# Hybrid decoder layer on one core: first loads in another order and on other queues, and the last token block's closing arithmetic on other engines

## The chip, the cores and the metric

The kernel runs on one core of a Trainium2 chip. A core has a matrix engine (TensorE, in the profile PE, with its weight loads listed as PEld), a vector engine (VectorE, DVE), an activation engine (ScalarE, ACT), a general engine (GpSimd, POOL) and a queue engine (SyncE, SP). SP, ACT and POOL can each issue DMA transfers; in the profile an issue stands under SPq, ACTq or POOL, and the queues that carry the packets are q1 (SP), q10 (ACT) and q0 (POOL). The metric is device time in microseconds (us), lower is better, as the median of several executions. One further execution is profiled, and all rows of the profile come from that one.

## What is computed

One layer on x of 512 tokens by 1024 channels, float32: a half-step SwiGLU feed-forward (2816 hidden channels), a mixer (RG-LRU channels beside sliding-window attention), and a second half-step feed-forward. Each is wrapped in RMS norms, one on its input and one on its output before the residual add:

```
def rms_norm(x, g):
    y = x * rsqrt(mean(x * x, axis=-1) + 1e-6)
    return y * g
def swiglu(x, w_gu, w_down):
    gate, up = split(x @ w_gu, 2)
    return (silu(gate) * up) @ w_down
x = x + 0.5 * rms_norm(swiglu(rms_norm(x, ffn1_pre_g), ffn1_w_gu, ffn1_w_down), ffn1_post_g)
x = x + rms_norm(mixer(rms_norm(x, mix_pre_g)), mix_post_g)
x = x + 0.5 * rms_norm(swiglu(rms_norm(x, ffn2_pre_g), ffn2_w_gu, ffn2_w_down), ffn2_post_g)
```

Only two places matter here: the first products of the first feed-forward (gate and up, with the gain `ffn1_pre_g`), and the output norm of the last feed-forward with its residual add, for the last 128 tokens.

## The kernel before

Each float32 operand of a product is split into a high part (rounded to the matrix engine's fast float32 form) and a low part (what the rounding left), and each product is three matmuls: high by high, low by high, high by low. The low-by-low one is left out. ACT makes most high parts (`act.copy`, a CAST in the profile), DVE most low parts (a subtraction, TENSOR_TENSOR), POOL a few. Every engine works through its own list in the order in which the code writes it; there is no scheduler that moves instructions, so one late instruction holds everything behind it on its engine.

**The head** (the first 15 us). x comes in as tiles `xn[b][hf]` of 128 tokens by 512 channels (b is the token block, hf the channel half), 256 KB each. PE turns them (transposes through an identity matrix that POOL builds), so that channels lie on partitions: `turn_early` turns the first channel half of blocks 0 and 1 (channel chunks 0 to 3), `turn(0, 4)` and `turn(0, 6)` the second half (chunks 4 to 7). From the turned data in the accumulation memory, `turned_high` makes x's high parts times the gain (xh), `turned_low` the low parts (xl, line 644). The gain is loaded as eight rows of 128 (`g1rows`) and turned by one small matmul (`g_ps`, line 1216), then copied by DVE (line 1282). The root of the mean square is applied later, so the products need only x and the gain.

The weights of the first gate column block (o = 0) and the first up column block (o = F) are loaded as four tiles of 256 KB, `first{o}{i}`, where i = 0 has channel chunks 0 to 3 and i = 1 chunks 4 to 7. The order's names number them: first_88 is gate chunks 0 to 3, first_91 (first_93 after the change) up chunks 0 to 3, first_96 gate 4 to 7, first_98 up 4 to 7. `first_hi` makes their high parts (line 1252, ACT), `first_lo` the low ones (line 1256, DVE, and POOL for the last). `passes(js, ks, part, xpart)` (line 1289) issues the products: js = 0 gate, 1 up; ks the chunks; `lower` is chunks 0 to 3, `upper` 4 to 7. PE's order is: 7 warm-up matmuls (`spin(WARM)`), the early transposes, `spin(2)`, the gate products on the lower chunks, the transposes of the second channel half, the gate's low-x products, the up products on the lower chunks (high, low x, low weight), then all products on the upper chunks. Then blocks 2 and 3 follow in the same way.

A transfer's completion is counted on one of eight semaphores, taken in turn over all transfers that SP and ACT issue. The ninth transfer therefore waits at its issue until the first has landed, the tenth for the second, and so on; the rows of the order show it as a wait on DMAHW0 to DMAHW7.

**The body** (15 to 806 us): feed-forward one, mixer, and feed-forward two, whose weights stream in over SP.

**The tail** (the last 20 us). For each block of 128 tokens, `out_products` ends the down product; DVE adds the part sums (`yp`, line 2126); ACT squares and sums over a row (line 2133, for the last piece line 2129); `tot` collects the mean squares, ACT takes the root (line 2139), DVE the reciprocal `rs` (line 2145); `last` is y times the gain (lines 2136 and 2141); and line 2148 makes the output, `last` times `rs` plus x. The last block has its second channel half in two pieces of 256 channels (i = 1 and 2), so that the last matmuls leave less to do behind them. The output goes out in three transfers for the last block: 256 KB (SP), 128 KB (ACT), 128 KB (SP).

## Time and profile before

| what | us |
|---|---|
| three runs | 835.01, 835.22, 835.38; median 835.22 |
| the profiled execution's own time | 836.39 |
| its span, first to last instruction | 834.6 |
| PE busy | 826.2 (99%) |
| DVE, ACT, POOL busy | 733.8, 520.0, 165.5 |
| mean granted clock of PE | 0.999 |

The profiled execution took 1.2 us longer than the median of the three runs, and 1.8 us of its own time lie outside the span. A row of the timeline gives start and duration in us, engine, line, operation, the tile written and the tiles read, sizes and a count of merged instructions; in square brackets stands how long the engine had been idle and what ended that. A merged row's duration reaches from the first instruction's start to the last one's end, and neighbouring rows of one engine may overlap by the pipeline. PE's records show one instruction per pass: a warm-up matmul has two, a transpose one.

### The profile page before, as it was taken

How to read it: one execution, taken by the hardware profiler on the slowest of the kernel's cores; microseconds unless marked ns; L12 is line 12 of the kernel's file. 1: busy time of each engine (PE TensorE's matmuls, PEld its weight loads, DVE VectorE, ACT ScalarE, POOL GpSimd, SP SyncE). 2: the span in 40 equal slices, each digit the busy share in tenths (PEclk: the TensorE clock that was granted, in tenths of full speed). 3: DMA queues.
4: the chain of work that ended last, by engine and by line, in shares of the span. 5: the costliest groups of instructions: out<-in, count | busy, mean ns of one | idle time of the engine just before them, and what ended most of it. 6: DMA issues, size and time to landing. Idle time of an engine off the chain costs nothing.

```text
span 834.6 us, 11761 instructions
## 1 busy us (share of the span) xinstructions
PE 826.2 (99%) x4190; PEld 701.0 (84%) x4190; DVE 733.8 (88%) x1031; ACT 520.0 (62%) x813; POOL 165.5 (20%) x187
## 2 busy tenths in 40 slices
...
GB/s 254 103 252 244 159 12 308 89 266 259 127 260 180 186 281 230 188 78 94 164 45 51 51 138 15 124 179 253 128 107 240 308 96 250 233 161 261 298 139 102
DMA packets 121835, 144.22 MB, mean 173 GB/s; under 512 B 24168, under 2 KB 76720, under 8 KB 121264
## 3 DMA queue, kind: packets, MB, share of 16 engines
...
q14 instruction: 26, 0.21, 0.1%
HBM read 100.45 MB, written 39.32 MB: 167 GB/s over the span
## 4 chain that ended last, share of the span: by engine, by line
PE 98%; DMA 1%; DVE 0%; SPq 0%; issue 0%; DVEq 0%
PE ab L1026 10%; PE aa L1026 10%; PE db L1026 5%; PE da L1026 5%; PE yaa L1427 3%; PE bb L1026 3%; PE ya L1427 3%; PE ba L1026 3%; PE a_first L1289 3%; PE yda L1427 2%; PE aa L956 1%; PE yab L2016 1%; PE yab L2017 1%; PE yab L2018 1%; PE wo L1942 1%; PE gt L522 1%
## 5 line engine op out<-in xcount | busy, mean ns | idle before, releaser
L1198 POOL DMA_DIRECT2D yr_a<-stage x36 | 31.2, 1015 | 175.7 <-ACT stage L1195 153.8
L1198 POOL DMA_DIRECT2D yp_b<-stage x42 | 36.5, 1070 | 146.3 <-ACT stage L1195 120.0
...
L745 POOL TENSOR_TENSOR acca_r<-acca_r,sq_r 128x512 f32<-128x512 f32 x6 | 9.1, 1509 | 38.2 <-ACT sq_r L552 38.1
L540 PE MATMUL an<-xh_mx,whi_xl 128*128 128x256 f32 x64 | 15.7, 285 | 0.0
L541 PE MATMUL an<-xh_mx,wlo_xl 128*128 128x256 f32 x64 | 15.5, 283 | 0.0
L2136 POOL TENSOR_TENSOR last<-yp,grow 128x512 f32<-128x512 f32 x3 | 3.9, 1291 | 57.0 <-DVE yp L2126 57.0
L2133 ACT ACTIVATE ysq<-yp 128x512 f32<-128x512 f32 (+1 forms) x8 | 4.9, 607 | 15.7 <-DVE yp L2126 15.7
L522 PE MATMUL gt<-xh_mx,whi_gt 128*128 128x512 f32 x32 | 14.2, 443 | 0.0
L1464 POOL DMA_DIRECT2D yp_a<-zy x16 | 8.7, 554 | 25.5 <-DMA rows_a<-yr_a 17.2
L498 ACT ACT_TABLE_LOAD x9 | 11.5, 1283 | 2.4 <-issue 2.3
L522 PE MATMUL pq<-xh_mx,whi_q 128*128 128x512 f32 x32 | 12.8, 400 | 0.0
L524 PE MATMUL gt<-xh_mx,wlo_gt 128*128 128x512 f32 x32 | 12.6, 394 | 0.0
L522 PE MATMUL pgb<-xh_f,whi_bg 128*128 128x512 f32 x32 | 12.6, 393 | 0.0
L523 PE MATMUL gt<-xl_mx,whi_gt 128*128 128x512 f32 x32 | 12.5, 392 | 0.0
L524 PE MATMUL pq<-xh_mx,wlo_q 128*128 128x512 f32 x32 | 12.5, 391 | 0.0
L523 PE MATMUL pq<-xl_mx,whi_q 128*128 128x512 f32 x32 | 12.5, 390 | 0.0
L524 PE MATMUL pgb<-xh_f,wlo_bg 128*128 128x512 f32 x32 | 12.5, 390 | 0.0
L524 PE MATMUL pub<-xh_f,wlo_bu 128*128 128x512 f32 x32 | 12.5, 390 | 0.0
L523 PE MATMUL pub<-xl_f,whi_bu 128*128 128x512 f32 x32 | 12.5, 390 | 0.0
L522 PE MATMUL pub<-xh_f,whi_bu 128*128 128x512 f32 x32 | 12.5, 389 | 0.0
L523 PE MATMUL pgb<-xl_f,whi_bg 128*128 128x512 f32 x32 | 12.5, 389 | 0.0
...
## 6 DMA issues: line engine op xcount, KB each, us to landing
...
raw_ad<-in_ffn_w_down SPq DMA_DIRECT2D x2, 1024.0 KB
xT_hbm<-xT POOLq DMA_DIRECT2D x2, 1024.0 KB, 6.1
```

The source lines that it names most:

```text
L498: act.activation(dummy, eps, func)
L522: pe.matmul(ps, hi[:, k, :], xh, start=start, stop=False)
L523: pe.matmul(ps, hi[:, k, :], xl, start=False, stop=False)
L524: pe.matmul(ps, lo[:, k, :], xh, start=False, stop=stop)
L540: pe.matmul(ps[:, sl], hi[:, k, :], xh, start=k == 0 and not goes_on, stop=False, skip_group_check=True)
L541: pe.matmul(ps[:, sl], lo[:, k, :], xh, start=False, stop=False, skip_group_check=True)
L745: eng.tensor_add(acc, acc, square(part, ALL, f"{self.name}{c}"))
L1026: pe.matmul(b[tb], x[:, blk], w[:, k, :], start=first and q + k + j == 0, stop=q + k == 2 and j == 2, skip_group_check=True)
L1198: pool.dma_start(o, st, accum_op=ALU.add)
L1289: pe.matmul(banks[j][:, sl], ws[j][part][:, k, :], n1.xs[k][xpart][:, sl], start=k == 0 and part == xpart, stop=stop and k == KD - 1)
L1427: pe.matmul(o, x[:, blk], a[:, k, :], start=start and j == 0, stop=stop and j == 2, skip_group_check=True)
L1464: (pool if q % 2 else sync).dma_start(chunks[32 * q:32 * (q + 1), :, i * P:(i + 1) * P], turned[32 * i:32 * (i + 1), :, q])
```

## The change

In the head, x's second channel half for blocks 0 and 1 is loaded over SP and ACT (one tile each) ahead of the up weights' lower chunks, and these are split into two transfers over both queues. The gain's rows leave SP's queue and are issued by POOL after it has built the identity. The gain's small matmul stands after the first two transposes, not after four; the spin behind the transposes is one matmul, not two. The first pair of xh moves from ACT to DVE, and the low part of the up weights' lower chunks from DVE to POOL.

In the tail, for the last block alone: the last piece's square and sum moves from ACT to DVE (a multiplication with a row sum as second output); the small `tot` step that needs only the first piece is written ahead of the last add; the last piece's gain product moves from DVE to POOL; its scaling with `rs` goes to ACT and its residual add to POOL, where one DVE instruction did both.

```diff
--- before.py
+++ after.py
@@ -449,10 +449,9 @@
     load_x(0, 0)
     load_x(1, 0, act)
     load_first(0, 0, act, sync)
-    load_first(F, 0, act)
-    sync.dma_start(g1rows, rows_of("ffn1_pre_g"))
-    for b in range(2):
-        load_x(b, 1)
+    load_x(0, 1)
+    load_x(1, 1, act)
+    load_first(F, 0, act, sync)
     for o in (0, F):
         load_first(o, 1, sync)
     for hf in range(2):
@@ -482,6 +481,7 @@
     dve.memset(ones.bitcast(F32), 1.0)
     ident = const.tile([P, P], F32, name="ident")
     make_identity(nc, ident)
+    pool.dma_start(g1rows, rows_of("ffn1_pre_g"))
 
     def filled(name, w, value):
         t = const.tile([P, w], F32, name=name)
@@ -1212,7 +1212,7 @@
             for i in range(2):
                 j = cc % 2
                 pe.transpose(tp[cc // 2][:, (2 * j + i) * P:(2 * j + i + 1) * P], xn[i][0][:, cc * P:(cc + 1) * P], ident)
-            if cc == 1:
+            if cc == 0:
                 pe.transpose(g1_ps[:, :KD], g1rows, ident[:KD, :KD])
         return dict(zip((0, 2), tp))
 
@@ -1280,7 +1280,7 @@
     g1_ps = bank("g1_ps")
     tps = turn_early()
     dve.tensor_copy(g1, g1_ps[:, :KD])
-    spin(2)
+    spin(1)
     banks = [bank(f"a_first{i}") for i in range(4)]
 
     def passes(js, ks, part=0, xpart=0, stop=False, sl=HALF[0]):
@@ -1298,7 +1298,7 @@
 
     preload(AF.Copy)
     first_hi(0, 0)
-    turned_high(0, 0, tps[0])
+    turned_high(0, 0, tps[0], dve)
     turned_high(0, 2, tps[2])
     first_lo(0, 0)
     turned_low(0, 0, tps[0])
@@ -1311,7 +1311,7 @@
     first_hi(1, 0)
     first_hi(0, 1)
     turned_high(0, 4, tps[4])
-    first_lo(1, 0)
+    first_lo(1, 0, pool)
     first_lo(0, 1)
     turned_high(0, 6, tps[6], dve)
     first_hi(1, 1)
@@ -2123,11 +2123,12 @@
         for i, (dh, c0, c1) in enumerate(pieces[tb]):
             out_products(tb, i, range(f0 + 2 * ((tb, i) in started), f1))
             y = parts[tb, dh][:, c0:c1]
+            if i == 2:
+                dve.tensor_scalar(tot, ss[:, 0:1], 4.0 / D, 4 * EPS, op0=ALU.mult, op1=ALU.add)
             dve.scalar_tensor_tensor(y, place(tb, i), -1.0 if dh else 1.0, y, op0=ALU.mult, op1=ALU.subtract if dh else ALU.add)
             if i == 2:
                 ss_last = small.tile([P, 1], F32, tag="tot", name="ss_last")
-                act.activation(wt(f"ysq{tb}{i}")[:, :c1 - c0], y, AF.Square, accum_out=ss_last)
-                dve.tensor_scalar(tot, ss[:, 0:1], 4.0 / D, 4 * EPS, op0=ALU.mult, op1=ALU.add)
+                dve.scalar_tensor_tensor(wt(f"ysq{tb}{i}")[:, :c1 - c0], y, 1.0, y, op0=ALU.mult, op1=ALU.mult, accum_out=ss_last)
                 dve.scalar_tensor_tensor(tot, ss[:, 1:2], 4.0 / D, tot, op0=ALU.mult, op1=ALU.add)
             else:
                 act.activation(wt(f"ysq{tb}{i}")[:, :c1 - c0], y, AF.Square, accum_out=ss[:, i:i + 1])
@@ -2138,14 +2139,20 @@
         if end:
             act.activation(rs, ss_last, AF.Sqrt, bias=tot, scale=4.0 / D)
             for i, (dh, c0, c1) in list(enumerate(pieces[tb]))[1:]:
-                dve.tensor_mul(last[i], parts[tb, dh][:, c0:c1], grow[dh][:, c0:c1])
+                (dve, pool)[i - 1].tensor_mul(last[i], parts[tb, dh][:, c0:c1], grow[dh][:, c0:c1])
         else:
             dve.tensor_add(tot, ss[:, 0:1], ss[:, 1:2])
             act.activation(rs, tot, AF.Sqrt, bias=eps4, scale=4.0 / D)
         dve.reciprocal(rs, rs)
+        if end:
+            act.activation(last[2], last[2], AF.Copy, scale=rs)
         for i, (dh, c0, c1) in enumerate(pieces[tb]):
             y = parts[tb, dh][:, c0:c1]
-            dve.scalar_tensor_tensor(y, last[i], rs, x_rows[tb][:, dh * T + c0:dh * T + c1], op0=ALU.mult, op1=ALU.add)
+            xr = x_rows[tb][:, dh * T + c0:dh * T + c1]
+            if i == 2:
+                pool.tensor_add(y, last[i], xr)
+            else:
+                dve.scalar_tensor_tensor(y, last[i], rs, xr, op0=ALU.mult, op1=ALU.add)
             (act if end and i == 1 else sync).dma_start(out[0, tb * P:(tb + 1) * P, dh * T + c0:dh * T + c1], y)
```

The first transfers of the two queues, before: eight of SP's rows, then ACT's first four (xn_77 and xn_79 are the first channel half of blocks 0 and 1, xn_78 and xn_80 the second half, xn_81 block 2).

```order
L440 DMA xn_77<-in_x 128x512
L447 DMA first_88<-in_ffn_w_gu 128x2x128
L453 DMA rows<-in_ffn_pre_g 8x128
L440 DMA xn_78<-in_x 128x512
L440 DMA xn_80<-in_x 128x512
L447 DMA first_96<-in_ffn_w_gu 128x4x128 [waits DMAHW0_49]
L447 DMA first_98<-in_ffn_w_gu 128x4x128 [waits DMAHW1_49]
L440 DMA xn_81<-in_x 128x512 [waits DMAHW2_49]
L440 DMA xn_79<-in_x 128x512
L447 DMA first_88<-in_ffn_w_gu 128x2x128
L447 DMA first_91<-in_ffn_w_gu 128x4x128
L498 ACT_TABLE_LOAD
```

And now, seven of SP's rows and ACT's first five:

```order
L440 DMA xn_77<-in_x 128x512
L447 DMA first_88<-in_ffn_w_gu 128x2x128
L440 DMA xn_78<-in_x 128x512
L447 DMA first_93<-in_ffn_w_gu 128x2x128
L447 DMA first_96<-in_ffn_w_gu 128x4x128 [waits DMAHW0_49]
L447 DMA first_98<-in_ffn_w_gu 128x4x128 [waits DMAHW1_49]
L440 DMA xn_81<-in_x 128x512 [waits DMAHW2_49]
L440 DMA xn_79<-in_x 128x512
L447 DMA first_88<-in_ffn_w_gu 128x2x128
L440 DMA xn_80<-in_x 128x512
L447 DMA first_93<-in_ffn_w_gu 128x2x128
L498 ACT_TABLE_LOAD
```

The second half of x stands ahead of the up weights on both queues, and the gain's rows have gone from SP's.

DVE's list in the head from the gain's copy on, before:

```order
L1282 COPY g_165<-g_ps 128x8 [waits PE_49]
L1256 TENSOR_TENSOR wlo_first_167<-first_88,whi_first_166 128x512 [waits DMAHW3_49,DMAHW2_49,Activation_49]
L644 SCALAR_TENSOR_TENSOR xl_a_148<-xtp_179,g_165,xh_a_147 128x256 [waits DVE_49,Activation_49]
L644 SCALAR_TENSOR_TENSOR xl_a_154<-xtp_180,g_165,xh_a_153 128x256
L1256 TENSOR_TENSOR wlo_first_169<-first_91,whi_first_168 128x512 [waits DMAHW4_49,Activation_49]
L1256 TENSOR_TENSOR wlo_first_167<-first_96,whi_first_166 128x512 [waits DMAHW0_49,Activation_49]
L1233 TENSOR_SCALAR xh_a_159<-xtp_221,g_165 128x256 [waits PE_49]
```

And now (two xl rows between the two shown are left out in both), with the two POOL rows that follow the identity:

```order
L1282 COPY g_166<-g_ps 128x8 [waits PE_49]
L1233 TENSOR_SCALAR xh_a_148<-xtp_180,g_166 128x256 [waits DVE_49,PE_49]
L1233 TENSOR_SCALAR xh_a_150<-xtp_180,g_166 128x256
L1256 TENSOR_TENSOR wlo_first_168<-first_88,whi_first_167 128x512 [waits DMAHW3_49,DMAHW2_49,Activation_49]
L644 SCALAR_TENSOR_TENSOR xl_a_149<-xtp_180,g_166,xh_a_148 128x256 [waits DVE_49]
L644 SCALAR_TENSOR_TENSOR xl_a_155<-xtp_181,g_166,xh_a_154 128x256
L1256 TENSOR_TENSOR wlo_first_168<-first_96,whi_first_167 128x512 [waits DMAHW0_49,Activation_49]
L1233 TENSOR_SCALAR xh_a_160<-xtp_221,g_166 128x256 [waits PE_49]
L484 DMA rows<-in_ffn_pre_g 8x128
L1256 TENSOR_TENSOR wlo_first_170<-first_93,whi_first_169 128x512 [waits DMAHW7_49,DMAHW6_49,Activation_49]
```

Two xh instructions came in ahead of the first low part, and the low part of the up weights has left DVE for POOL.

DVE's last rows, before:

```order
L2126 SCALAR_TENSOR_TENSOR yp_7721<-ybl_7899,yp_7721 128x256 [waits PE_49]
L2130 TENSOR_SCALAR tot_b_8037<-ss_b_8036 128x1 [waits Activation_49]
L2131 SCALAR_TENSOR_TENSOR tot_b_8037<-ss_b_8036,tot_b_8037 128x1 [waits DVE_49,Activation_49]
L2141 TENSOR_TENSOR last_8070<-yp_7721,grow_7725 128x256
L2141 TENSOR_TENSOR last_8089<-yp_7721,grow_7725 128x256
L2145 RECIPROCAL rs_b_8090<-rs_b_8090 128x1 [waits Activation_49]
L2148 SCALAR_TENSOR_TENSOR yp_7717<-last_8053,rs_b_8090,x_rows_7834 128x512 [waits DVE_49]
L2148 SCALAR_TENSOR_TENSOR yp_7721<-last_8070,rs_b_8090,x_rows_7834 128x256
L2148 SCALAR_TENSOR_TENSOR yp_7721<-last_8089,rs_b_8090,x_rows_7834 128x256
```

And now DVE's last rows, then ACT's one and POOL's two new ones:

```order
L2128 SCALAR_TENSOR_TENSOR yp_7721<-ybl_7899,yp_7721 128x256 [waits PE_49]
L2131 SCALAR_TENSOR_TENSOR ysq_8086,ss_last<-yp_7721 128x256 [waits DVE_49]
L2132 SCALAR_TENSOR_TENSOR tot_b_8037<-ss_b_8036,tot_b_8037 128x1 [waits Activation_49]
L2142 TENSOR_TENSOR last_8070<-yp_7721,grow_7725 128x256
L2146 RECIPROCAL rs_b_8090<-rs_b_8090 128x1 [waits Activation_49]
L2155 SCALAR_TENSOR_TENSOR yp_7717<-last_8053,rs_b_8090,x_rows_7834 128x512 [waits DVE_49]
L2155 SCALAR_TENSOR_TENSOR yp_7721<-last_8070,rs_b_8090,x_rows_7834 128x256
L2148 ACTIVATE last_8089<-last_8089,rs_b_8090 128x256 [waits DVE_49,Pool_49]
L2142 TENSOR_TENSOR last_8089<-yp_7721,grow_7725 128x256 [waits DMAHW3_49,DVE_49,Activation_49]
L2153 TENSOR_TENSOR yp_7721<-last_8089,x_rows_7834 128x256 [waits DMAHW6_49,PE_49,Activation_49]
```

DVE takes the square on and gives up one gain product and one output instruction; the last piece passes from POOL to ACT and back to POOL.

## The prediction

> **What bounds the kernel now.** I read the page's busy shares and chain first, then PE's waits, then the timeline of the first 16 and the last 8 us.
>
> ```profile
> PE 826.2 (99%) x4190; PEld 701.0 (84%) x4190; DVE 733.8 (88%) x1031; ACT 520.0 (62%) x813; POOL 165.5 (20%) x187
> PE 98%; DMA 1%; DVE 0%; SPq 0%; issue 0%; DVEq 0%
> PE xtp L1224 <- DMA xn<-in_x: 0.8, 2, 0.5
> ```
>
> PE is the bound, and beside its start it waits for one thing only: x's second half, in the head. From there to its last matmul it is never idle, so there is nothing to win in the body; what is won is a shorter way to that unbroken run, and a shorter way from its end to the last transfer.
>
> ```profile
> 4.27 1.08 PE L1214 MATMUL xtp<-ident,xn 128*128 128x128 f32 x4
> 5.28 0.27 PE L1216 MATMUL g_ps<-ident,rows 8*128 8x8 f32 x1
> 5.49 1.11 PE L1214 MATMUL xtp<-ident,xn 128*128 128x128 f32 x4
> 6.39 0.86 PE L1277 MATMUL warm<-ones 128*128 128x128 f32 x4
> 7.00 0.91 PE L1289 MATMUL a_first<-xh_a,whi_first 128*128 128x256 f32 x4
> 7.75 0.64 PE L1289 MATMUL a_first<-xh_a,wlo_first 128*128 128x256 f32 x4
> 8.64 0.33 PE L1224 MATMUL xtp<-ident,xn 128*128 128x128 f32 x1 [0.25 <-DMA xn<-in_x]
> 9.52 0.98 PE L1224 MATMUL xtp<-ident,xn 128*128 128x128 f32 x7 [0.55 <-DMA xn<-in_x]
> 10.26 0.72 PE L1289 MATMUL a_first<-xl_a,whi_first 128*128 128x256 f32 x4
> 15.24 1.91 PE L1224 MATMUL xtp<-ident,xn 128*128 128x128 f32 x16
> ```
>
> See three things. The gain's matmul comes late (5.28) and two spin matmuls (four records from 6.39) fill the time to 7.00. The low products end near 8.2 and the low-x products start at 10.26, though the eight transposes between them need less than 1 us: the rest is the wait for x. And spacing halves on the way: a transpose takes 0.22 us in the four from 5.49 to 6.39, and 0.11 in the seven from 9.52 to 10.26; 256 columns take 0.12 from 7.75 on.
>
> **The head, part by part.** *The gain.* POOL issues it when the identity is done, at 1.37. No transfer by POOL stands so early in the trace; the nearest rows are its later ones:
>
> ```profile
> 1.08 0.29 POOL masks.py:199 TENSOR_SCALAR_AFFINE_SELECT ident<-ident 128x128 f32<-128x128 f32 x1
> yp_a<-zy POOLq DMA_DIRECT2D x16, 64.0 KB, 2.6
> xT_hbm<-xT POOLq DMA_DIRECT2D x2, 1024.0 KB, 6.1
> ```
>
> The gain is 4 KB, so I take the smaller: landed by 1.4 + 2.6 = 4.0; the far end is 1.4 + 6.1 = 7.5. PE asks for it after two transposes, 4.27 + 2 x 0.21 = 4.70. With it there, PE does the small matmul to 4.91, six transposes to 6.19, one spin (two records) to 6.61: the first product starts 0.39 earlier than at 7.00.
>
> *Its inputs.* First gate weights land at 5.14 and ACT has them rounded at 5.76:
>
> ```profile
> 5.14 0.62 ACT L1252 CAST whi_first<-first 128x512 fp32r<-128x512 f32 x1 [1.36 <-DMA first<-in_ffn_w_gu]
> 5.79 1.69 ACT L641 ACTIVATE xh_a<-xtp,g 128x256 fp32r<-128x256 f32 x4
> 16.76 0.88 DVE L1233 TENSOR_SCALAR xh_a<-xtp,g 128x256 fp32r<-128x256 f32 x2 [2.65 <-PE xtp L1224]
> ```
>
> Before, ACT made four xh one after another to 7.48, which held the fourth product. Now DVE makes two (0.44 each, from 5.4, when the first bank is turned) and ACT two to 6.9, so all eight gate products run from 6.61 without a gap, the first at the slow spacing, and end at 8.0 in place of 8.2. The low part moves behind the two xh on DVE, to 7.1, and is wanted at 7.5. The one spin less costs nothing by itself: PE's spacing changed near 7.7 and PE stays busy up to there.
>
> *x's second half.* Now 512 KB over two queues, right behind the first gate weights and ahead of the up weights. Before, in the half microsecond from 4.5, ACT's queue moved up weights and SP's, where x stood, almost nothing:
>
> ```profile
> q10 hardware_dynamic: 184, 0.09, 61.1%
> q1 hardware_dynamic: 6, 0.00, 1.1%
> ...
> q10 hardware_dynamic: 51, 0.10, 54.5%
> q1 hardware_dynamic: 44, 0.09, 48.2%
> ```
>
> The columns are packets, MB and the share of the 16 engines' time; the second pair is the half microsecond from 2.5, when both queues moved x's first halves. From 5.14, 512 KB at those 0.19 MB per half microsecond take 1.4 us: landed near 6.5, at the latest 8.0 if they lag as before. Either way PE, at 8.0, finds it. Eight transposes (0.11 each) end at 8.9, and the low-x products start there: 1.35 earlier than 10.26. The low parts of x are ready (DVE: four of 0.43 from 7.1 to 8.8).
>
> *What is late next.* Behind these products PE wants the up weights, then both weights' upper chunks. Before, these were a chain on ACT, DVE and POOL that began when the up weights landed:
>
> ```profile
> SPq L440 <- DMA first<-in_ffn_w_gu: 3.4, 1, 3.4
> 9.70 1.33 ACT L1252 CAST whi_first<-first 128x512 fp32r<-128x512 f32 x2 [2.22 <-DMA first<-in_ffn_w_gu]
> 10.35 1.40 DVE L1256 TENSOR_TENSOR wlo_first<-first,whi_first 128x512 fp32r<-128x512 f32 x2 [1.96 <-ACT whi_first L1252]
> 10.94 0.83 ACT L641 ACTIVATE xh_a<-xtp,g 128x256 fp32r<-128x256 f32 x2
> 11.67 0.87 DVE L1233 TENSOR_SCALAR xh_a<-xtp,g 128x256 fp32r<-128x256 f32 x2
> 12.36 1.30 POOL L1256 TENSOR_TENSOR wlo_first<-first,whi_first 128x512 fp32r<-128x512 f32 x1 [10.98 <-ACT whi_first L1252]
> ```
>
> The up weights (256 KB in small packets) now come behind x. Earliest 6.5 + 0.7 = 7.2 (0.09 MB in half a microsecond and up), latest the old 9.65; half-way is 8.4. Then ACT rounds to 9.0, POOL's low part (1.30 where DVE took 0.70) ends at 10.36, and PE, which wants them at 9.4 and 10.36, just gets them. Next ACT takes the upper gate chunks. Their landing cannot be read: by 10.41 they were there, since ACT took them, as the second of the two from 9.70, without a wait. Taking 9.1 (ACT free) to 10.41, half-way 9.75: rounded at 10.4, ACT's two xh to 11.2, the last upper weights to 11.8; DVE's low part to 11.1 and its two xh to 11.9. PE would start the upper products at 10.85 and needs the last xh at 11.2: 0.7 late; POOL's last low part, 11.85 to 13.15, comes about as wanted. So the head ends 0.65 earlier than before: I take **0.7**. With the upper chunks at 9.1 it is 1.3; with everything as late as before it is 0. What is queued behind POOL's new instruction is only that last low part.
>
> The body passes the gain on: SP's issues wait for earlier landings, so x's later tiles are issued sooner (the 3.4 us wait above goes), and where ACT waits for a later weight PE has work:
>
> ```profile
> 29.39 1.05 ACT L210 CAST whi_au<-raw_au__380 128x1024 fp32r<-128x1024 f32 x1 [1.75 <-DMA raw_au__380<-in_ffn_w_gu]
> ```
>
> ACT stood idle for 1.75 us there and PE's list of waits has nothing for it; a shift of 0.7 fits under that cover. If it did not, the head's term would shrink towards 0, the first rival's value.
>
> **The tail.** PE ends near 828.1; then:
>
> ```profile
> 828.13 0.42 DVE L2126 SCALAR_TENSOR_TENSOR yp<-ybl,yp 128x256 f32<-128x256 f32 x1 [0.18 <-PE ybl L1994]
> 828.59 0.42 ACT L2129 ACTIVATE ysq<-yp 128x256 f32<-128x256 f32 x1
> 828.91 0.19 ACT L2129 ACTIVATION_READ_ACCUMULATOR ysq<-yp 128x1 f32 x1
> 829.07 0.16 DVE L2131 SCALAR_TENSOR_TENSOR tot_b<-ss_b,tot_b 128x1 f32<-128x1 f32 x1 [0.46 <-DVE tot_b L2130]
> 829.14 0.75 DVE L2141 TENSOR_TENSOR last<-yp,grow 128x256 f32<-128x256 f32 x2
> 829.32 0.29 ACT L2139 ACTIVATE rs_b<-ss_last,tot_b 128x1 f32<-128x1 f32 x1 [0.23 <-DVE tot_b L2131]
> 829.82 0.16 DVE L2145 RECIPROCAL rs_b<-rs_b 128x1 f32<-128x1 f32 x1
> 830.01 1.54 DVE L2148 SCALAR_TENSOR_TENSOR yp<-last,rs_b,x_rows 128x512 f32<-128x512 f32 x3
> 831.07 0.48 DVE L2148 SCALAR_TENSOR_TENSOR yp<-last,rs_b,x_rows 128x256 f32<-128x256 f32 x1
> L776 POOL TENSOR_TENSOR xT<-yp_a,xT 128x256 f32<-128x256 f32 x8 | 6.7, 839 | 6.3 <-DVE yp_a L772 5.9 <-DMA raw_q<-in_w_in 0.3
> ```
>
> The reciprocal waits for DVE's second gain product, not for ACT. The square on DVE has no row; between an output instruction of this size (0.48) and that plus ACT's 0.19 for reading the row sum, I take the lower, which is the nearer in kind. Then: square 828.57 to 829.05, `tot` to 829.2, root to 829.6, reciprocal to 829.8, first output from 829.8 in place of 830.01; DVE's outputs end at 830.9, not 831.55. The last piece: POOL's product (0.84) from 828.6 is done by 829.5, ACT scales to 830.25, POOL adds to 831.1. Behind ACT's scaling in its list stands the issue of the middle 128 KB; it is wanted only at 830.9, when DVE has that piece, so the scaling's wait for `rs` holds nothing up. So the issues come 0.2 (256 KB), 0.2 and 0.45 us earlier. The 512 KB need about 1.4 us on the engines in either case, so the end moves by a value between: **0.3**, bounds 0.1 (square with the extra 0.19) and 0.45.
>
> Sum against the profiled execution: 836.39 - 0.7 - 0.3 = 835.4. That execution lies 1.17 above the median of the runs, and I carry the difference: 835.22 - 1.0 = **834.2**.
>
> **Rivals.** *The landings are only dealt anew.* The second half of x comes early, but the same bytes have to pass before the upper chunks, and these land when they did. For it: the up weights landed 4.5 us after the first gate weights though little stood ahead of them. Against it: SP's queue stood nearly still from 4.5 to 5.0. Head 0, tail 0.3: **834.9**. [...]
>
> *Everything lands in time.* Head 1.3, tail 0.45: **833.5**. For it: the engines were at 62% in the half microsecond from 4.5 (61.1 and 1.1), so bytes could move sooner. Against it: ACT, DVE and POOL then have to work without a gap from 8.4 to 13.
>
> *The gain by POOL is late.* PE stands in order behind its small matmul. Each microsecond after 4.7 is one; with the gain at 7.5 the first product starts at 7.5 + 0.2 + 1.3 + 0.4 = 9.4, low-x at 11.3, 1.0 later than before; less the tail's 0.3, **835.9**. It decides from a landing at about 6.8. For it: no transfer of POOL's is seen this early, and larger ones take up to 6.1. Against it: the 64 KB row.
>
> *The square costs more than the product it replaces.* With its 256 columns at half speed on DVE (0.27 more: the first of the three outputs, of 512 columns, takes 0.74 of the 1.54, and 0.27 above 0.48) and the 0.19 for the row sum, the reciprocal comes 0.2 later than now: tail -0.2, **834.7**. For it: two inputs from SBUF take 0.48 where the add from the accumulation memory takes 0.42; that is far from half. [...]
>
> **Chances.** Forecast 0.42, dealt anew 0.23, all in time 0.20, gain late 0.07, square 0.08. A change below 0.2% (1.7 us) cannot be told from none here, so faster means under 833.55: 0.12 of the second rival's 0.20, which lies on that line, and 0.10 of the forecast's own case, together 0.22; slower (over 836.9) needs the gain later than any row of its size, 0.04; the rest, 0.74, is no change. The range runs from just past the best case to just past the median of before: 833.2 to 835.4.
>
> **What would show it.** The gain's matmul without a wait near 4.7; low-x products before 9.2; a new PE gap, if any, in the upper products behind DVE's xh or POOL's low part; the 16 transposes of blocks 2 and 3 near 14.5 in place of 15.24; PE's end as much earlier; the reciprocal near 829.6 less that shift. A wait of PE for the gain, or up weights landing after 9.6, would prove me wrong.

## The result, and the profile after

The changed kernel takes 840.13 us (median of six runs, 838.53 to 841.39) where the kernel before takes 835.35 (six runs, 835.01 to 835.43). The ratio is 1.0059, with a 95% interval of 1.0046 to 1.0072: the change costs 4.8 us, and the times of the changed kernel spread over 2.9 us where those of the kernel before spread over 0.4. Forecast were 834.2 us and a range of 833.2 to 835.4.

The profiled execution of the changed kernel took 838.53 us with a span of 836.8. It is the fastest of the six, while the profiled execution before (836.39) lies above all six of its runs, so the spans of the two profiles differ by 2.2 us only. TensorE's list of waits in the changed kernel, which before named only the start and 0.8 us for x:

```profile
PE g_ps L1216 <- DMA rows<-in_ffn_pre_g: 2.3, 1, 2.3
...
PE cur L1724 <- DVE home L1613: 0.2, 1, 0.2
```

The wait for x is gone. In its place stands one for the gain, three times as long, and one in the middle of the program. The chain of waits of the changed kernel in the head (start, length, what) shows where the first comes from:

```profile
1.56 5.34 DMA rows<-in_ffn_pre_g
...
6.94 0.22 PE g_ps L1216
```

GpSimd issues the gain at 1.56, and it is there at 6.90: 5.34 us for 4 KB. Before, by SP's queue, the gain's matmul started at 5.28. The chain begins at GpSimd's identity and runs through this transfer; nothing else in the head is on it until TensorE has the gain.

The wait has a second price. TensorE in two stretches of 3.4 us in the changed kernel; the columns are the stretch and its length, TensorE's busy time and matmuls, the granted clock, the share of the DMA engines and GB/s:

```profile
4.00:7.41 3.41, 1.13 (x9) 1.00 1.06 329
7.41:10.83 3.42, 3.42 (x18) 0.50 1.08 383
```

In the stretch with the wait TensorE works 1.13 of 3.41 us; in the whole next one half the clock is granted (0.50), and the first products are 0.21 us apart in place of 0.12. The granted clock changes at 7.41 and at 10.83 in this record, 3.42 us apart, and the gap in the stretch ahead, the wait for the gain, is 2.28 us long.

What follows in the head was as forecast: neither the eight transposes of x's second half (from 10.54) nor ACT's two roundings of up weights (from 9.14) wait for a transfer. But they start late. The sixteen transposes of blocks 2 and 3 begin at 16.34 in place of 15.24, and this 1.1 us goes on unchanged to the mixer, near 404. There the changed kernel (first fence) and the kernel before (second) part again:

```profile
396.90 1.30 SPq L1585 DMA_DIRECT2D ig<-other  x1
...
403.28 1.60 POOL L1587 TENSOR_TENSOR xc<-ig,xc 128x512 f32<-128x512 f32 x1
403.66 2.31 DVE L215 TENSOR_TENSOR wlo_gt<-raw_gt__3749,whi_gt 128x1024 fp32r<-128x1024 f32 x1
405.89 0.28 DVE L1613 TENSOR_TENSOR home<-pq,R_mx 128x128 f32<-128x128 f32 x1
```

```profile
395.80 0.53 SPq L1585 DMA_DIRECT2D ig<-other  x1
...
402.35 1.21 DVE L215 TENSOR_TENSOR wlo_gt<-raw_gt__3749,whi_gt 128x1024 fp32r<-128x1024 f32 x1
402.53 2.17 POOL L1587 TENSOR_TENSOR xc<-ig,xc 128x512 f32<-128x512 f32 x1 [0.66 <-DMA ig<-other]
403.48 0.28 DVE L1613 TENSOR_TENSOR home<-pq,R_mx 128x128 f32<-128x128 f32 x1
```

One issue on SP takes 1.30 us in place of 0.53. GpSimd's next steps shift against VectorE's, so that GpSimd's product starts ahead of VectorE's low part and no longer behind it; and now it is VectorE that takes twice its time (2.31 for 1.21), where before GpSimd took 2.17 for 1.60. `home` comes 2.41 later while the program runs 1.1 later here, TensorE waits, and 0.5 us more are lost. Then VectorE and GpSimd in the tail of the changed kernel:

```profile
829.71 0.42 DVE L2128 SCALAR_TENSOR_TENSOR yp<-ybl,yp 128x256 f32<-128x256 f32 x1
830.16 0.42 DVE L2131 SCALAR_TENSOR_TENSOR ysq<-yp 128x256 f32<-128x256 f32 x1
830.26 0.91 POOL L2142 TENSOR_TENSOR last<-yp,grow 128x256 f32<-128x256 f32 x1 [5.85 <-ACT ysq L2134]
830.51 0.08 DVE L2131 DVE_READ_ACCUMULATOR ysq<-yp 128x1 f32 x1
830.51 0.67 DVE L2132 SCALAR_TENSOR_TENSOR tot_b<-ss_b,tot_b 128x1 f32<-128x1 f32 x1
...
831.54 0.16 DVE L2146 RECIPROCAL rs_b<-rs_b 128x1 f32<-128x1 f32 x1
831.74 1.65 DVE L2155 SCALAR_TENSOR_TENSOR yp<-last,rs_b,x_rows 128x512 f32<-128x512 f32 x2
832.39 0.72 POOL L2153 TENSOR_TENSOR yp<-last,x_rows 128x256 f32<-128x256 f32 x1 [1.22 <-ACT last L2148]
```

The square costs what was assumed (0.42, and 0.08 for its row sum). But the sum over one column behind it takes 0.67 us where it took 0.16, and ends with GpSimd's product (830.26 + 0.91 = 831.17); and the two outputs take 1.65 where the first two took 1.15, beside GpSimd's addition. From the last addition's start the reciprocal comes after 1.83 us, before after 1.69. The span ends 7.39 us behind the start of TensorE's last product (829.39), before 6.75 (827.81). So the pair divides into 1.1 us head, 0.5 body, 0.6 tail.

### The profile page after: what moved, and what is told of

It is laid out like the page before. It is cut to its first block, busy times and chain, and to the rows that moved or that the text cites. A ratio compares the mean times of both kernels' runs of the same rounds, so it can differ in the third digit from the quotient of the medians.

```text
span 836.8 us, 11763 instructions
## 1 busy us (share of the span) xinstructions
PE 826.1 (99%) x4188; PEld 701.3 (84%) x4188; DVE 735.3 (88%) x1032; ACT 519.0 (62%) x810; POOL 168.1 (20%) x191
## 4 chain that ended last, share of the span: by engine, by line
PE 94%; DVE 3%; DMA 1%; ACT 1%; issue 1%; POOL 0%; DVEq 0%; POOLq 0%
PE ab L1026 10%; PE aa L1026 10%; PE db L1026 5%; PE da L1026 5%; PE yaa L1427 3%; PE a_first L1289 3%; PE bb L1026 3%; PE ba L1026 3%; PE ya L1427 3%; PE yda L1427 2%; PE aa L956 1%; PE yab L2016 1%; PE yab L2018 1%; PE yab L2017 1%; PE wo L1942 1%; DVE xc L1572 1%
```

## The experiments

Each median stands beside that of the kernel before, run 21 to 33 times alongside. Ratios stand with their 95% interval; where it holds 1, the time alone decides nothing, and what is said rests on the rows of one profile. The spread is the highest run less the lowest. The kernel before has 1.0 to 2.6 us of it in these larger groups, with the middle half of its runs within 0.5 us, so a spread is worth something only beside the bulk of the runs.

Three numbers of each profile carry most of what follows: the start of the sixteen transposes of blocks 2 and 3 (the head's end), the start of TensorE's last product, and the span. The body is the second less the first, the tail the third less the second.

| profile | head's end | body | tail | time of that execution |
|---|---|---|---|---|
| before | 15.24 | 812.57 | 6.75 | 836.39 |
| the change | 16.34 | 813.05 | 7.39 | 838.53 |
| the change again | 18.60 | 813.00 | 7.40 | 840.74 |
| change with spins | 17.86 | 812.65 | 7.39 | 839.66 |
| before, gain by GpSimd | 17.01 | 812.69 | 6.50 | 838.01 |
| change, gain on SP | 15.25 | 813.02 | 7.63 | 837.72 |
| head alone, gain on SP | 15.01 | 814.07 | 7.54 | 838.53 |
| the same, split 3:1 | 14.45 | 813.09 | 7.54 | 837.07 |
| the same, TensorE's list as before | 14.39 | 812.64 | 7.52 | 836.45 |
| before, one spin less | 14.53 | 813.08 | 6.79 | 836.23 |
| before, one load more | 13.92 | 812.56 | 7.53 | 835.84 |
| before, new tail | 14.57 | 812.68 | 6.94 | 836.21 |
| before, square on VectorE | 13.99 | 812.70 | 6.61 | 835.13 |
| before, last piece on GpSimd | 14.62 | 812.76 | 6.82 | 836.23 |
| before, product moved | 15.42 | 812.64 | 6.40 | 836.29 |
| eight loads, product moved | 14.55 | 812.72 | 6.39 | 835.66 |
| the same, low part on VectorE | 14.15 | 812.56 | 6.40 | 834.94 |

### The gain's queue

Before, with only the gain moved:

```
-    sync.dma_start(g1rows, rows_of("ffn1_pre_g"))
     make_identity(nc, ident)
+    pool.dma_start(g1rows, rows_of("ffn1_pre_g"))
```

> The kernel before with one thing done: the gain goes by GpSimd's queue. Theory G: it lands at 6.9 or later in place of 5.28 or before, PE waits for it 1.6 us or more, the granted clock falls for a stretch behind that idle time, and since PE waited 0.8 us for x's second half anyway, the end comes 0.8 to 3.5 later: 836.2 to 838.9, spread over 1 us. Theory W: 835.4, no change.

Measured: 838.98 against 835.79, ratio 1.0037 (1.0025 to 1.005), spread 1.6 us. Its list of transfers (KB, and us from issue to landing), and TensorE by stretches as above:

```profile
rows<-in_ffn_pre_g POOLq DMA_DIRECT2D x1, 4.0 KB, 5.9
```

```profile
5.09:8.50 3.41, 1.21 (x12) 1.00 0.97 298
8.50:11.91 3.41, 3.41 (x17) 0.50 1.05 372
```

The same picture as in the changed kernel, with the old order of everything else: 5.9 us to the landing, a stretch with 1.21 us of work, then a stretch at half the clock (0.50 for 3.41 us). This one line of the change costs 3.2 us. Theory W fell for this part.

The change with the gain put back on SP's queue:

```
-    pool.dma_start(g1rows, rows_of("ffn1_pre_g"))
     load_first(0, 0, act, sync)
+    sync.dma_start(g1rows, rows_of("ffn1_pre_g"))
```

> The changed kernel with one thing undone: the first norm's gain (4 KB) goes by SP's queue again, behind the first gate weights, in place of GpSimd's. Theory G (the gain's late landing is what costs the head: 5.34 us from issue in the profile of the change, PE idle 2.3 us, then a stretch at half the granted clock; and it lands later still in other executions, which is the spread of 2.9 us): PE's wait at the gain is gone, the head comes 0.7 earlier than in the kernel before, the tail costs 0.65 as in the profiled pair: 835.35 - 0.7 + 0.65 = 835.3, spread under 1 us. Theory W (the new order of x and weights, or PE's new list, is what costs the head): still 838.5 or more, and a spread of about 3 us.

Measured: 837.39 against 835.79, ratio 1.0023 (1.0012 to 1.0033), spread 3.05 us. From the other side the gain's queue is again worth some 3 us, but theory G's 835.3 is missed: 1.6 us remain, and the spread with them. So the gain is not all of the loss, and the runs still scatter without it (836.20 to 839.25 in seven).

The changed kernel itself again:

> The changed kernel itself once more, on the chip of the experiments, for a second profile. Theory G (the gain by GpSimd's queue, and the clock that falls behind the idle time): 4 to 5 above the kernel before; PE's wait at the gain 2.3 us or more, a stretch of 3.4 us at half the granted clock right behind it; a slower execution shows a longer wait or a stretch that lies worse. Rival (the first chip was peculiar): 1.4 above, the sum of the head with the gain on SP (0.85) and the tail (0.5).

Measured: 840.74 against 835.90, ratio 1.0049 (1.0035 to 1.0063). This profile is of an execution at the median, and its head is 2.3 us worse than in the first profile. The list of transfers and TensorE's timeline in the head (start, length, instruction; merged rows give the whole length):

```profile
rows<-in_ffn_pre_g POOLq DMA_DIRECT2D x1, 4.0 KB, 6.4
```

```profile
7.99 0.27 PE L1216 MATMUL g_ps<-ident,rows 8*128 8x8 f32 x1 [3.08 <-DMA rows<-in_ffn_pre_g]
8.19 1.54 PE L1214 MATMUL xtp<-ident,xn 128*128 128x128 f32 x6
9.81 1.43 PE L1289 MATMUL a_first<-xh_a,whi_first 128*128 128x256 f32 x4
...
11.89 1.91 PE L1224 MATMUL xtp<-ident,xn 128*128 128x128 f32 x8
13.46 0.99 PE L1289 MATMUL a_first<-xl_a,whi_first 128*128 128x256 f32 x4
```

The gain landed 1.1 us later (6.4 against 5.3), and the slow spacing lasted longer: eight transposes take 1.91 us, where seven took 0.98 in the kernel before, and the four low-x products 0.99 for 0.72. The granted clock does not show this: it reads 1.00 from 8.00 to 14.00, where theory G has half, and 0.999 over this execution (0.996 over the first profile's). It reads 1.00 in the kernel before too, from 3.40 to 6.80, where four transposes are 0.22 apart. So a half clock in this execution is the author's estimate from the spacing (0.21 for 0.12). The landing took 5.3, 5.9 and 6.4 us in the three profiles so far; it varies, and with it the place and the length of the idle time. That this is the head's part of the spread is likely, but shown by these few profiles only.

How much are the slow matmuls behind the wait? The change with sixteen spins (32 records) ahead of the gain's transpose, so that TensorE works while it waits:

```
             if cc == 0:
+                spin(16)
                 pe.transpose(g1_ps[:, :KD], g1rows, ident[:KD, :KD])
```

> The changed kernel with sixteen spins ahead of the gain's transpose, which keep TensorE at work for 1.7 to 3.4 us while the gain is under way; the gain's landing is as it was. Theory C (a part of the loss is the clock: half of it granted for 3.4 us or more behind the idle time, products 0.21 apart in place of 0.12): full clock from about 7 on, 0.8 to 1.5 under the changed kernel, so 3.3 to 4 above the kernel before. Rival (all is the landing): 4.8 above, or more where the spins themselves come late.

Measured: 839.14 against 835.83, ratio 1.0043 (1.003 to 1.0056), 1.5 us less over the kernel before than the change itself just above (3.3 against 4.8; two groups of runs, so this is a rough difference). TensorE's timeline and the transfer:

```profile
4.70 4.83 PE L1278 MATMUL warm<-ones 128*128 128x128 f32 x32
9.46 0.23 PE L1217 MATMUL g_ps<-ident,rows 8*128 8x8 f32 x1
9.62 0.88 PE L1214 MATMUL xtp<-ident,xn 128*128 128x128 f32 x6
```

```profile
rows<-in_ffn_pre_g POOLq DMA_DIRECT2D x1, 4.0 KB, 6.2
```

The spins overran: the gain was there at about 1.55 + 6.2 = 7.75, and TensorE took it at 9.46. Though it started 1.5 us later than in the profile just above (7.99), the head ended 0.74 earlier (17.86 for 18.60), as six transposes take 0.88 in place of 1.54 and so on. By this comparison the slow matmuls behind the wait are worth some 2.2 us in such an execution. Theory C's time holds (3.3 to 4 above the kernel before), and the matmuls behind the gain are fast again; a granted clock of 0.50 behind the wait stands in two profiles (the changed kernel's first, and the gain alone) and not in the one at the median. But the spins also moved the instruction packet (below), and the body is back at 812.65, so 0.35 of the 1.5 us is the body's.

### The rest of the head

The kernel before with the change's head, the gain on SP, the tail as it was:

```
-    load_first(F, 0, act)
     sync.dma_start(g1rows, rows_of("ffn1_pre_g"))
-    for b in range(2):
-        load_x(b, 1)
+    load_x(0, 1)
+    load_x(1, 1, act)
+    load_first(F, 0, act, sync)
...
-            if cc == 1:
+            if cc == 0:
...
-    spin(2)
+    spin(1)
-    turned_high(0, 0, tps[0])
+    turned_high(0, 0, tps[0], dve)
-    first_lo(1, 0)
+    first_lo(1, 0, pool)
```

> The kernel before with the change's head (x's second half on both queues ahead of the up weights, DVE and GpSimd taking a part each, one spin less), but with the gain on SP's queue, and the old tail. Theory G: 835.35 - 0.7 = 834.6 (834.0 if every landing is in time). Theory W: 838 or more less the tail, with the spread. A third, that landings are only dealt anew: 835.3, nothing gained.

Measured: 836.64 against 835.79, ratio 1.001 (1.0001 to 1.0019), spread 2.4. Theory G's 834.6 is missed: even with the gain on SP this head costs 0.85. Its profile has all three reasons in it that the next runs take apart: TensorE still waits 0.7 us for the gain, asked for two transposes earlier, and the first four products take 1.43 as in the changed kernel (0.91 in the kernel before), though the granted clock reads 1.00 here; the body is 814.07; and the tail, though it is the old one, is 7.54.

With TensorE's list as before (the gain behind four transposes, two spins), the rest as in that run:

```
-            if cc == 0:
+            if cc == 1:
...
-    spin(1)
+    spin(2)
```

> The kernel of the run with the head alone (gain on SP), with TensorE's list as it was: the gain's transpose behind four transposes in place of two, and two spins. Theory C (TensorE's full clock comes 2.2 us later with the change's list, near 9.1 in place of 6.9, since it stands idle 0.7 us for the gain in the stretch from which the clock is granted): products 0.12 apart from 7 us on, low-x products near 9.4 in place of 10.1, 0.7 under the run with the head alone, so about 0.1 to 0.2 above the kernel before (the loss in the mixer stays). Rival (x's second half sets the low-x products, the clock nothing): 0.85 above the kernel before, as that run.

Measured: 836.02 against 835.76, ratio 1.0004 (0.9995 to 1.0013), spread 1.2: 0.6 less than with the change's list, near the 0.7 of theory C, though the interval allows more and less; the granted clock reads 1.00 in the heads of both, so what these two profiles show is the spacing alone. The low-x products start at 8.74, earlier than the forecast's 8.9. But not all of the 0.6 is the spacing's: the loss in the mixer, which C's sum kept, is gone too (body 812.64).

With up weights dealt three chunks to ACT and one to SP:

```
-    load_first(F, 0, act, sync)
+    load_first(F, 0, act, sync, ks=(3, 1))
```

> The kernel of the run with the head alone (gain on SP), with one thing changed: of the first up weights ACT takes three chunks of 128 rows and SP one, in place of two and two, so that SP's queue carries as many packets in the head as in the kernel before. Theory R (one of SP's issues in the middle of the program, the load of ig near 396, takes 1.2 to 1.4 us in all three kernels with the new head and 0.5 in all three with the old, because the queue's count of packets decides which issue has to wait; DVE's and GpSimd's work in the mixer then collide and PE loses 0.4 to 1.4 us): the issue is back at 0.53, PE waits nowhere between 20 and 820 us, and the time is 0 to 0.3 under the kernel before of the same call. Rival (chance, or the shifted phase): as with two and two, 0.85 above the kernel before.

Measured: 836.76 against 835.76, ratio 1.0014 (1.0005 to 1.0023). The issue takes 1.22 us, TensorE waits 0.2 in the mixer: theory R, by SP's packets, fell. This profile also limits theory C: with the change's list and a wait of 0.5 us for the gain, the six transposes behind it take 0.88, as behind the spins, where the run with the head alone took 1.54. And a later profile with TensorE's old list (before, product moved) waits 0.6 us for the gain and is still slow behind it (1.05 for four products in place of 0.64). So TensorE's list alone does not decide the spacing; behind a short wait the matmuls are slow in some executions and not in others. Of the kernels so far, those with one spin and the gain behind two transposes had the long issue, those with TensorE's old list had not, whatever their loads were. That led to the next run.

### The loss in the body

Before, with one spin less and nothing else:

```
-    spin(2)
+    spin(1)
```

> The kernel before with one thing taken away: one of the two spins behind the first transposes. Theory F (a block of PE's instructions is fetched at a fixed count of them; with the change's list the fetch falls on SP's issue of the load of ig near 396, which then takes 1.2 to 1.4 us in place of 0.53; it does so in all four kernels with the list of the change and in none of the six with the old one): the issue takes 1.2 or more, DVE's home comes late, 0.2 to 1.4 above the kernel before. Rival (it is the place of the gain's transpose, or chance): issue at 0.53, no wait of PE between 20 and 820, the same as before.

Measured: 836.77 against 835.90, ratio 1.0011 (1.0002 to 1.0019), spread 2.9 us (835.25 to 838.14). SP's issue in its timeline:

```profile
395.10 1.28 SPq L1585 DMA_DIRECT2D ig<-other  x1
```

One matmul pair taken out at 7 us makes an SP issue at 395 take 1.28 us, makes TensorE wait 0.2 us for VectorE's `home` as in the changed kernel, and scatters the runs: five of its eleven lie above 836.9, of the 27 of the kernel before one. Theory F puts this down to an instruction packet, and the traces bear it out in place and time. The queues' packets (count, MB, share) from just ahead of that issue on, in the changed kernel the row of instructions from 396.85 to 397.9, in the kernel before all rows from 395.75 to 396.85:

```profile
q8 instruction: 1, 0.02, 5.7%
```

```profile
q1 hardware_dynamic: 51, 0.10, 41.9%
q0 software_dynamic: 3, 0.00, 2.6%
```

A packet of 16 KB of instructions passes in the changed kernel and none in the kernel before. Over the profiles, with starts from each trace:

| profile | instruction packet | issue | length of the issue |
|---|---|---|---|
| before | 394.56 | 395.80 | 0.53 |
| TensorE's list as before | 393.67 | 394.99 | 0.52 |
| one spin less | 395.04 | 395.10 | 1.28 |
| the change | 396.87 | 396.90 | 1.30 |
| the change again | 399.13 | 399.16 | 1.28 |
| split 3:1 | 394.84 | 395.07 | 1.22 |

All six profiles with one spin (these four, the change with the gain on SP 1.18, the head alone 1.39) have packet and issue within 0.25 us of each other and a long issue; in all ten with two spins the packet comes 1.1 to 1.5 us ahead and the issue takes 0.52 to 0.54; with 32 spin records more there is no packet near it. The coincidence and its dependence on TensorE's count of instructions are shown; what inside the queue holds the issue is not. What follows is the same in all six: GpSimd's product starts ahead of VectorE's low part, which takes 2.30 to 2.31 us; in all eleven other profiles it takes 1.21. The body grows by 0.35 to 0.5 us in five of the six and by 1.4 in one (814.07), where a second wait follows. Such second waits may be the body's part of the spread; one profile is too little to show it.

### The tail

Before, with the whole new tail (the tail's part of the change's diff):

> The kernel before with the change's tail alone. Theory T (the tail's loss in the profiled pair is real: a root 0.14 later, GpSimd's addition beside DVE's outputs, the last write 0.25 later): 835.35 + 0.65 = 836.0, spread as before. Rival as in the prediction (the tail gains 0.3, what the pair shows is chance): 835.05. Third (the tail carries what the profiled pair does not explain, and the spread): 838 or more.

Measured: 836.32 against 835.79, ratio 1.0006 (0.9997 to 1.0015). By the medians the tail is a loss of 0.53, not a gain of 0.3, and the interval just holds 1. By its rows it is less: the tail is 6.94 in place of 6.75, and the last packet of the output passes 5.46 us behind the start of TensorE's last product in place of 5.31.

Before, with the square alone (the last piece stays on VectorE):

```
+            if i == 2:
+                dve.tensor_scalar(tot, ss[:, 0:1], 4.0 / D, 4 * EPS, op0=ALU.mult, op1=ALU.add)
...
-                act.activation(wt(f"ysq{tb}{i}")[:, :c1 - c0], y, AF.Square, accum_out=ss_last)
-                dve.tensor_scalar(tot, ss[:, 0:1], 4.0 / D, 4 * EPS, op0=ALU.mult, op1=ALU.add)
+                dve.scalar_tensor_tensor(wt(f"ysq{tb}{i}")[:, :c1 - c0], y, 1.0, y, op0=ALU.mult, op1=ALU.mult, accum_out=ss_last)
```

> The kernel before with the tail's first half of the change alone: the last square on VectorE, and its first sum ahead of the last addition; the last piece stays on VectorE. Theory P (what costs in the tail is GpSimd's two operations, each of which holds one of VectorE's: 0.67 in place of 0.16 at the sum, and about 0.5 at the second output): the root comes 0.1 to 0.2 earlier or later, time within 0.2 of the kernel before. Rival S (the square with its row sum costs): 0.5 above it, as with the whole new tail.

Before, with the last piece alone on GpSimd and ACT (the square stays on ACT):

```
-                dve.tensor_mul(last[i], parts[tb, dh][:, c0:c1], grow[dh][:, c0:c1])
+                (dve, pool)[i - 1].tensor_mul(last[i], parts[tb, dh][:, c0:c1], grow[dh][:, c0:c1])
+        if end:
+            act.activation(last[2], last[2], AF.Copy, scale=rs)
...
+            if i == 2:
+                pool.tensor_add(y, last[i], xr)
```

> The kernel before with the tail's second half of the change alone: the last piece's product and addition on GpSimd and its scaling on ACT; the square stays on ACT. Theory P: GpSimd's product (0.91) holds the sum or the product on VectorE by about 0.4, its addition the second output by 0.5: 0.3 to 0.6 above the kernel before. Rival S: the same as before or 0.2 to 0.4 under it, since VectorE has one output and one product less.

Measured: the square alone 835.54, the last piece alone 835.82, against 835.76: ratios 0.9996 (0.9987 to 1.0005) and 1.0002 (0.9993 to 1.0011). Neither can be told from no change by time; the rows tell them apart. The sum over one column with the square alone, and then with the last piece alone, with GpSimd's product beside it (with both, it is as in the changed kernel above):

```profile
827.82 0.15 DVE L2132 SCALAR_TENSOR_TENSOR tot_b<-ss_b,tot_b 128x1 f32<-128x1 f32 x1
```

```profile
828.25 0.72 POOL L2141 TENSOR_TENSOR last<-yp,grow 128x256 f32<-128x256 f32 x1 [5.85 <-ACT ysq L2133]
828.63 0.36 DVE L2131 SCALAR_TENSOR_TENSOR tot_b<-ss_b,tot_b 128x1 f32<-128x1 f32 x1 [0.46 <-DVE tot_b L2130]
```

Without GpSimd 0.15; beside it the sum ends where GpSimd's product ends, within 0.02 us (828.99 and 828.97; in the changed kernel 831.18 and 831.17). It is not the square but GpSimd at the same time that costs. In the mixer too it is the one that starts second that takes longer: VectorE's low part behind GpSimd's product (2.31 for 1.21) in the changed kernel, GpSimd's product behind VectorE's low part (2.17 for 1.60) in the kernel before. What the two contend for no run shows.

In the kernel before, VectorE stands idle for 0.46 us ahead of that sum, and a product can go there. Before, with the middle piece's product moved into it:

```
+            if i == 2:
+                dve.tensor_scalar(tot, ss[:, 0:1], 4.0 / D, 4 * EPS, op0=ALU.mult, op1=ALU.add)
...
                 act.activation(wt(f"ysq{tb}{i}")[:, :c1 - c0], y, AF.Square, accum_out=ss_last)
-                dve.tensor_scalar(tot, ss[:, 0:1], 4.0 / D, 4 * EPS, op0=ALU.mult, op1=ALU.add)
+                dve.tensor_mul(last[1], parts[tb, pieces[tb][1][0]][:, pieces[tb][1][1]:pieces[tb][1][2]], grow[pieces[tb][1][0]][:, pieces[tb][1][1]:pieces[tb][1][2]])
                 dve.scalar_tensor_tensor(tot, ss[:, 1:2], 4.0 / D, tot, op0=ALU.mult, op1=ALU.add)
...
-            for i, (dh, c0, c1) in list(enumerate(pieces[tb]))[1:]:
+            for i, (dh, c0, c1) in list(enumerate(pieces[tb]))[2:]:
```

> The kernel before with one thing done in the tail, and the old head: the first sum ahead of the last addition, and the middle piece's gain product moved into VectorE's wait for ACT's square (0.46 us idle in the profile). The reciprocal comes 1.33 us behind the start of the last addition in place of 1.69: 0.3 under the kernel before. If the head of the version before this one gave something, this one is 0.1 or more above that (which was 0.38 under the kernel before); if the whole gain was the tail's, the two are the same. Rival: the end hangs on the writes, not on the reciprocal, and nothing is gained.

Measured: 835.42 against 835.83, ratio 0.9996 (0.9987 to 1.0005). The reciprocal comes 1.32 us behind the start of the last addition, as expected, and the tail is 6.40 in this profile and in both others that have the moved product, against 6.75 and 6.79 in the two with the old tail and eight loads. But the run with the gain by GpSimd, whose tail is the old code, reads:

```profile
830.60 0.16 DVE L2131 SCALAR_TENSOR_TENSOR tot_b<-ss_b,tot_b 128x1 f32<-128x1 f32 x1
```

There VectorE does not stand idle ahead of the sum, the reciprocal comes after 1.34 us, and the last packet passes after 4.95, as with the moved product (4.94). So the idle time is no wait for ACT's square: in the kernel before, ACT had read the sum that this step needs at 828.55, and the step starts at 829.07. What it is no row shows, and whether the moved product fills it or only moves VectorE's list out of its way is open.

### The end of the program

Before, with one small load more on ACT's queue that nobody reads:

```
     load_first(F, 0, act)
+    act.dma_start(rows_t[:KD, 2 * P:3 * P], rows_of("ffn1_pre_g"))
```

> The kernel before with one thing added: a ninth transfer by a hardware queue in the head, 4 KB on ACT's queue behind the first up weights, that nobody reads. Theory L (at the end SP waits for one completion counter after the other in a fixed order; the counters are dealt in turn to the transfers, and with one transfer more the last write's counter comes third in the list in place of last, so that the rest of the list, some 0.8 us, is walked after the write has landed; this is in all runs with the gain on SP): 0.77 above the kernel before, and the time from PE's end to the span's end 7.5 in place of 6.5 to 6.75. Rival (the walk costs nothing, or hangs on the loads' order): the same as before within 0.2.

Measured: 836.13 against 835.90, ratio 1.0003 (0.9994 to 1.0012). The mechanism shows in the profile, the sum does not show in the time. SP's waits at the end of this kernel, then of the kernel before:

```profile
SPq L2175 <- DMA out_dram<-yp: 1.6, 1, 1.6
```

```profile
SPq L2174 <- DMA out_dram<-yp: 0.7, 2, 0.4
```

The tail is 7.53 in place of 6.75. The last packets of the last write pass 5.3 us behind the last product's start in both; the rest, 2.23 against 1.45, is SP's list. At the end of the kernel before SP runs through ten waits from 831.96 to 833.67, nine of them for two counters, and the last write's counter stands in the tenth. Here, by the author's reading of the one wait of 1.6 us, it stands in the third, and the other seven, 0.8 us with the step to the end, come after it. All five profiles with nine loads by hardware queues in the head have tails of 7.5 to 7.6. But the head of this profile is among the earliest (13.92), and the medians differ by 0.23 where 0.77 was expected: whether nine loads also help the head, since SP's later issues then wait for other counters, or chance has made it up, is open.

The changed kernel has eight loads, and yet its tail is 7.39 where the new tail alone has 6.94. Its last packet passes as early (5.46 in both). What is longer is a wait of SP at the very end, when the engines wait for one another (the row names TensorE's queue), first in the changed kernel, then with the new tail alone:

```profile
SPq L2181 <- PEq L2181: 1.1, 2, 0.9
```

```profile
SPq L2181 <- PEq L2181: 0.7, 2, 0.5
```

In the first, GpSimd's last closing step starts 0.5 us behind the one before it, in the second 0.2. The longer wait (0.8 or 0.9) stands in the four profiles with the change's head and tail together, and 0.5 in the thirteen others; why is open.

### Two versions from the parts

The first: new order of x's second half, up weights in one transfer on ACT (eight loads), gain on SP, TensorE's list as before, and the product moved in the tail. The second: the same, with one low part of the weights back from GpSimd on VectorE:

```
-    first_lo(1, 0, pool)
+    first_lo(1, 0)
```

> A version made of what has shown itself so far: x's second half on both queues ahead of the up weights, the up weights in one transfer on ACT (so that there are eight transfers by hardware queues, as before), the gain on SP, TensorE's list as before, DVE's and GpSimd's parts as in the change; in the tail the square stays on ACT, the first sum goes ahead of the last addition, and one of VectorE's two products moves into its wait for the square. From the run with TensorE's list as before (0.26 above): less 0.77 for the counters, less 0.2 for the tail: 0.7 under the kernel before. Rival (the loads' new order gives nothing, the counters nothing): 0.05 above to 0.2 under.

> The version with eight loads, new order and the tail's product moved, with the first up weights' low part back on VectorE in place of GpSimd. Theory S (side by side, GpSimd's 1.30 us and VectorE's 1.09 in place of 0.69 slow each other, VectorE's parts of x come late and the upper products stretch from 1.12 to 1.62): VectorE's low parts take 0.7 each, upper products 1.12 to 1.2, and the program enters the body 0.2 to 0.5 earlier: 0.2 to 0.5 under that version. Rival (the upper weights land too late, or one engine with all low parts is later still): the same or 0.4 above it.

Measured: the first 835.52 against 835.90, ratio 0.9994 (0.9985 to 1.0003), no more than the moved product alone brings: its head gives nothing. The second 834.94 against 835.83, ratio 0.999 (0.9981 to 0.9999), spread 0.4: the only version that is faster than the kernel before by more than the interval, if barely. The head of the first version, and then of the second:

```profile
9.04 0.72 PE L1289 MATMUL a_first<-xl_a,whi_first 128*128 128x256 f32 x4
9.24 1.30 POOL L1256 TENSOR_TENSOR wlo_first<-first,whi_first 128x512 fp32r<-128x512 f32 x1 [7.87 <-ACT whi_first L1252]
10.00 1.09 DVE L1256 TENSOR_TENSOR wlo_first<-first,whi_first 128x512 fp32r<-128x512 f32 x1 [1.14 <-ACT whi_first L1252]
11.01 0.86 DVE L1233 TENSOR_SCALAR xh_a<-xtp,g 128x256 fp32r<-128x256 f32 x2
11.17 1.62 PE L1289 MATMUL a_first<-xh_a,whi_first 128*128 128x256 f32 x8
```

```profile
8.74 0.72 PE L1289 MATMUL a_first<-xl_a,whi_first 128*128 128x256 f32 x4
9.16 1.51 DVE L1256 TENSOR_TENSOR wlo_first<-first,whi_first 128x512 fp32r<-128x512 f32 x2 [0.60 <-ACT whi_first L1252]
10.58 0.87 DVE L1233 TENSOR_SCALAR xh_a<-xtp,g 128x256 fp32r<-128x256 f32 x2
10.74 1.63 PE L1289 MATMUL a_first<-xh_a,whi_first 128*128 128x256 f32 x8
```

In the first, VectorE's low part takes 1.09 beside GpSimd's. In the second both low parts take 1.51 together on VectorE, done at 10.67, and VectorE's parts of x follow 0.4 earlier. The upper products still stretch (1.63 for eight; 1.12 is their usual time), against theory S: they wait for VectorE's part of x either way. Of the 0.40 us by which this head ends earlier, 0.30 is there before the low part matters: the low-x products start at 8.74 in place of 9.04, as the eight early transposes take 0.60 and 0.66 here and 1.09 and 1.11 there. The granted clock of the first version reads 1.00 up to 8.00, so what slows them there no row shows. Some 0.1 us is left for the low part (0.24 against the run with TensorE's list as before, whose low-x products also start at 8.74).

## Why the prediction was wrong

**The gain's landing** is the step that failed most, and the wait for the gain is the sign that the prediction itself had named as proof against it. The prediction took 4.0 from a row of 2.6 us for 64 KB and kept 7.5 as the far end. It landed at 6.9 and, in the execution at the median, near 8.0 (1.55 + 6.4). The row was of a transfer in the body; this one stands among all the loads of the head. In the changed kernel's transfers no packet of GpSimd's queue passes before 5.1, and its 32 packets stand in the stretch from 5.1 to 6.6 among 540 of the two other queues (packets, MB, share of the engines' time):

```profile
q10 hardware_dynamic: 262, 0.29, 53.9%
q1 hardware_dynamic: 278, 0.20, 45.5%
q0 software_dynamic: 32, 0.00, 1.9%
```

So some 3.6 us pass from the issue to the first packet, 1.4 more until the last, and 0.3 to the landing. What holds the first packet back no run takes apart. The rival "the gain by POOL is late", with a chance of 0.07, was the right mechanism, and its point of decision (6.8) lies just below the measured landing. Its price was too low: it had the low-x products at 11.3 with a landing at 7.5, and they start at 11.47 with the landing at 6.9 and at 13.46 with the one near 8.0. It had no term for slow matmuls behind the wait, which is what lies between: the six transposes behind the gain took 1.28 and 1.54 us, where they take 0.88 behind the spins, and the first four products 1.43 in both, for 0.91 in the kernel before.

**The clock** was missing in all cases. The prediction read the spacing of transposes (0.22, then 0.11), but used it only to put the missing spin at no price; it did not ask what idle time would do to it. Half the clock was granted behind the idle time in two profiles (0.50 for 3.42 and 3.41 us); in that at the median the granted clock reads 1.00, and a half clock is only estimated from the spacing, which is slow for longer. The late landing and the slow matmuls together are what the run with the gain alone shows (3.2 us).

**The profiled execution.** The forecast's 0.7 from x's second half was taken from an execution that lay 1.0 us above the median, and the difference was carried as a constant. It was not one. Seven profiles with the old loads and the gain on SP end the head between 13.92 and 15.42, and the one that the prediction read stands second latest; three of the seven have no wait for x at all. What the new order could win was in good part a property of that execution. The rest of the step held where the gain is on SP and TensorE's list as before: x's second half and the up weights were in time, the low-x products start at 8.74 and 9.04 (8.9 was forecast), 0.65 to 0.8 us are then lost, most of it in the upper products behind VectorE's part of x, where the prediction had put 0.7, and the head ends at 14.39 and 14.55 (14.5 was forecast). The loss is what these two take from the low-x products to the head's end, 5.65 and 5.51 us, beyond the 4.87 of the changed kernel, where nothing waits on that way. There was luck in it. VectorE's low part took 1.09 to 1.14 us beside GpSimd's where 0.70 was counted, and began earlier than counted (9.80 for 10.4 in the run with TensorE's list as before). And the landing of the up weights, 8.4, came out in that run although its early bound, 7.2, goes by x's rate: at the 0.09 MB in half a microsecond that the prediction names beside it, 256 KB take some 1.5 us and not 0.7. So the new order ends the head where it was said to, but the old one ends it at 14.6 in the mean, and little is left to win.

**The body** was counted as passing the gain on unchanged. Its cover against a late weight held. What failed is "one spin less" at no price: with it an instruction packet passes just as SP issues a transfer in the mixer, and the body takes 0.35 to 0.5 us more in five profiles and 1.4 in one; alone it raised the median by 0.9 us.

**The tail.** The square's own price held, 0.42 us and 0.08 for its row sum, and the half speed that its rival counts with stands in no run (the square takes 0.42 where the product takes 0.41). With the square alone the reciprocal starts 1.55 us behind the last addition's start in place of 1.69, so 0.14 earlier where 0.2 was forecast; but against the 1.34 of the old tail without VectorE's unexplained idle time it is later, so this gain is not safe. The failed step is GpSimd's part, priced as if it ran beside VectorE at no cost: it holds VectorE's sum by 0.5 us and its second output by another 0.5 (1.65 for 1.15). By its rows the new tail alone brings the last packet 0.15 us later, where 0.3 earlier was forecast. Of the 0.64 in the first pair of profiles, 0.45 is the longer wait at the very end, which no arithmetic of the tail explains.

**The sum.** Gain by GpSimd +3.2 (measured alone), the rest of the head +0.85, tail +0.5: 4.6, against 4.8 measured both times. That it comes out so well is in part luck: the 0.85 was measured with nine loads and so has the longer walk at the end in it (tail 7.54), which the changed kernel with its eight has not; this has the 0.45 in its place. In the profile of the execution at the median the head ends 4.0 later than the seven old profiles' mean (14.6), the body takes 0.35 more and the tail 0.6.
